# A two-layer hybrid decoder trunk on one core: maxima turned by grouped matmuls, three VectorE steps moved to ScalarE, pair halves of the residual norms summed before the ones-matmul

## The chip, the cores and the metric

The kernel runs on one core of one Trainium2 chip. The metric is the device time of one execution in microseconds. Before the change it is 1284.84 us, the median of three runs (1284.32 to 1285.02). The trace comes from one more execution, with the hardware profiler on; it took 1287.62 us, of which 1285.9 us lie between its first and last instruction (the span).

Engine names are those of the profile: PE is TensorE's matrix product and PEld its weight load, DVE is VectorE, ACT is ScalarE, POOL is GpSimd, SP is SyncE.

## What is computed

One sequence of 512 tokens and 16 meta tokens (L = 528), width 1024, two layers, everything in fp32. Each layer has a mixer and a feed-forward part, each between two RMS norms:

```python
def mixer_sublayer(h, ...):
    u = rms_norm(h, pre_g)
    z = jnp.einsum("bld,de->ble", u, w_in)
    q, k, v, f_logit, a_val, a_gate, sc_b, sc_c, sc_x = jnp.split(z, idx, axis=-1)
    log_f = jax.nn.log_sigmoid(f_logit + b_forget)
    y_attn = forgetting_attention(q, k, v, log_f)      # 8 heads of 64, causal softmax in query blocks
    a = a_val * jax.nn.sigmoid(a_gate)
    a = causal_depthwise_conv(a, a_dw_w) + a_dw_b      # 31 taps, 256 channels
    a = jax.nn.silu(layer_norm(a, a_ln_g, a_ln_b))
    y_conv = jnp.einsum("blc,ce->ble", a, a_pw_w)
    y_sc = sc_b * causal_depthwise_conv(sc_c * sc_x, sc_conv_w)   # 3 taps
    y = jnp.concatenate([y_attn, y_conv, y_sc], axis=-1)
    y = jnp.einsum("ble,ed->bld", head_rms_norm(y, head_g), w_out)
    return h + rms_norm(y, post_g)

def ffn_sublayer(h, ...):
    u = rms_norm(h, pre_g)
    z = causal_depthwise_conv(jnp.einsum("bld,df->blf", u, w_up), conv_w)   # 3 taps
    g, up = jnp.split(z, 2, axis=-1)
    return h + rms_norm(jnp.einsum("blf,fd->bld", jax.nn.silu(g) * up, w_down), post_g)
```

## The kernel before

Activations lie with channels on the 128 partitions and time along the free axis, in two time halves of H = 264 (`half_sl`). Every large product is done in three passes of a rounded type (`mm3`, L675): high part of the weights by high part of the activations, high by low, low by high. Weights stream from HBM in blocks of 128 output columns; ScalarE makes the high part (L629, L477 and L498) and VectorE the low part (L633, L478, L499).

The order of the instructions on every engine is mostly made at build time by a planner, `Flow`. It keeps a virtual clock for each engine. Threads (Python generators) issue the matmuls, and operations of the other engines are queued with a duration (`act_us`, `dve_us`, `stt_us`), what they come after, and a priority; whichever can start first on the virtual clocks goes out next. The durations decide the order alone; on the chip each engine runs its list in order and waits on semaphores. So a change of the operations of one stage also reorders the matmuls of that stage. The middle of the feed-forward part lies outside the planner and is ordered by the tile framework.

Places that matter below:

- **Maxima** (`maxima`, L1393). For each of the 8 heads, scores of queries by keys are made once more (L1407) to find the row maxima: VectorE reduces each piece along the free axis into one column of `mcol` (L1414), one column for each of five query blocks (`QB`: 16 queries, then four of 128). A maximum then stands on a partition for each query; the exponentials need it along the free axis, as one extra row of q (`mrow`) that meets a row of ones in k. The column is turned by a matmul with the identity (L1431): one matmul for each block, four in a first group and one in a second. ScalarE copies each group with a factor of -1 into the row of q (L1434): 400 elements, then 128.
- **Exponentials** (`logits`, L1453): two matmuls of k by q for each piece, the first of which reads the row of maxima; ScalarE takes exp of the result (L1462).
- **Fill.** The thread `fill` keeps TensorE busy between these with the input projections (`proj` and `v_proj`, L675 and L1259), later with the first output products (`Early`).
- **Convolution** (`conv_taps`): 31 taps on VectorE for two channel blocks; the first is a multiply and add of a scalar (L988), the others L991.
- **Short convolution** (`sc_x`): three steps on VectorE, the first a multiplication (L1069), then L1071 twice.
- **Layer norm and silu** (`conv_tail`, `silu`): gain (L1596), bias (L1599, VectorE), exp (L1600, ScalarE), ln, exp, and a product (L1603).
- **Residual norms** (`Norms`). `square` adds squares of channel blocks, two at a time, into `acc`, a tile of two halves of a block each (L763 and L772). `factor` sums over channels by a matmul with a matrix of 1/1024, `om_d` (L812, plain fp32), once for each of the two halves of the pair; three ScalarE steps (L822, L825, L826) and two of VectorE (L827, L833) make the factor. Key "y" is the norm behind a sublayer, "h" the one ahead of the next; each has two time halves (0 and 1). `post_norm` scales (L889), adds to h (L899) and writes the next input in two parts (L904 on ScalarE, L906 on VectorE). In the last sublayer the second half of "y" has its last blocks kept apart (`alone`).

Of the kernel before, what the change touches and what calls it, by code (L numbers as in the profile page):

```python
# [15 lines left out]
P = 128  # L16
# [310 lines left out]
def stt_us(n):  # L327
    return 0.22 + 0.00102 * n
# [13 lines left out]
def tile_hybrid_trunk(ctx: ExitStack, tc: tile.TileContext, xT, wflat, pv_d, out):  # L342
# [35 lines left out]
    for l in range(DEPTH):  # L378
        pv = T(const, [P, NPV], F32, f"pv{l}")
        (nc.gpsimd if l else nc.sync).dma_start(pv, pv_d[l])  # L380
        pg = T(const, [P, NGAIN], F32, f"pg{l}")
        nc.vector.tensor_scalar_mul(pg, pv[:, :NGAIN], -0.5)
        pvs.append((pv, pg))

    ident_r = T(const, [P, P], F32R, "ident_r")
    ident = ident_r.bitcast(F32)
# [349 lines left out]
    class Norms:  # L736
# [17 lines left out]
        def square(self, key, k, src, n, *after, prio=1):  # L754

            apart = self.alone.get(key, self.apart.get(key[0], 0))
            s = self.sums.setdefault(key, {"parts": {}})
            us = act_us(2 * n)
            box, slot = {}, Slot()

            def squares(tile):
                box["c"] = tile()
                nc.scalar.activation(box["c"], src, AF.Square)  # L763

            if k == 0:
                a = act(us, lambda: squares(lambda: T(self.pool, [P, 2, H], F32, "acc", 2)[:, :, :n]), *after,
                        prio=prio, takes=[(self.acc, slot)])
                s["acc"], s["at"] = box, a
            else:
                a = act(us, lambda: squares(lambda: self.c_tile(n)), *after, prio=prio, takes=[(self.c, slot)])  # L770
                if k < KD - 2 * apart:
                    s["at"] = dve(dve_us(2 * n), lambda: nc.vector.tensor_add(s["acc"]["c"], s["acc"]["c"], box["c"]),  # L772
                                  a, s["at"], prio=prio)
                    slot.close(s["at"])
            if k == 0 or k >= KD - 2 * apart:
                s["parts"][max(0, k // 2 - KD // 2 + apart + 1) if k else 0] = box, slot
                box["at"] = [a]
            if k == KD - 2 * apart - 2:
                s["acc"]["at"], s["acc"]["there"] = [s["at"]], True
            return a  # L780

# [179 lines left out]
                first.slot[hf, 2 * j + i].close(a, d)  # L961

    def mixer(l, ypool, first, close_first, spans, front, rz0_at):
        pv, pg = pvs[l]

        def col(name, j):
            return pv[:, _COLS[name] + j:_COLS[name] + j + 1]
# [17 lines left out]
        def tap(j, i):  # L985
            src = apads[j][:, i:i + L]
            if i == 0:
                nc.vector.tensor_scalar(conv[j], in0=src, scalar1=col("a_dw_w", CK * j),  # L988
                                        scalar2=col("a_dw_b", j), op0=ALU.mult, op1=ALU.add)
# [71 lines left out]
        def sc_x(j):  # L1061
# [4 lines left out]

            def shift(i):
                if i == 2:
                    nc.vector.tensor_scalar(t, in0=cx[:, 2:], scalar1=col("sc_w", 3 * j + 2), scalar2=None, op0=ALU.mult)  # L1069
                else:  # L1070
                    nc.vector.scalar_tensor_tensor(t, in0=cx[:, i:i + L], scalar=col("sc_w", 3 * j + i), in1=t,  # L1071
                                                   op0=ALU.mult, op1=ALU.add)

            def use(hf, ps, tok, rz=None):
                c = half_sl(hf)
                got.append(dve(dve_us(H), lambda: nc.vector.tensor_mul(cx[:, 2 + H * hf:2 + H * (hf + 1)], ps, t[:, c]),
                               tok, sc_at[j, "c", hf], prio=0))
                if hf:
                    d = got
                    for i in (2, 0, 1):  # L1080
                        d = [dve(stt_us(L), lambda i=i: shift(i), *d, prio=3)]
                    sc_at[j, "x"] = d[0]
                return [got[-1]]

# [308 lines left out]
        def maxima():  # L1393

            for hd in range(HEADS):
                yield [When(lambda: k_at.get(hd)), When(lambda: q_at[hd] if hd // 2 in k2_at else None),
                       When(lambda: gate_at.get(hd))] + ([When(lambda: begun.get(hd - 1))] if hd else [])
                q1, k1 = qh[hd % 4][0], kh[hd % 4][0]
                mcol = T(mp, [P, 6], F32R, "mcol", 2)
                col_at = []  # L1400
                for b, (qs, n) in enumerate(QB):
                    end = qs + n
# [17 lines left out]
                        slot.close(d)  # L1420
                        yield
                    col_at.append(d)
                mrow = rows(hd)[2]
                at = []
                for group in (QB[:4], QB[4:]):
                    yield [col_at[QB.index(g)] for g in group]
                    ps, slot = yield from bank("s1")
                    c0, c1 = group[0][0], group[-1][0] + group[-1][1]
                    for qs, n in group:
                        b = QB.index((qs, n))  # L1430
                        nc.tensor.matmul(ps[:1, qs - c0:qs - c0 + n], lhsT=mcol[:n, b:b + 1],  # L1431
                                         rhs=ident_r[:n, :n], start=True, stop=True)
                    tok = flow.mm(0.07 * len(group))
                    at.append(act(act_us(c1 - c0), lambda ps=ps, c0=c0, c1=c1: nc.scalar.activation(  # L1434
                        q1[mrow, c0:c1], ps[:1, :c1 - c0], AF.Copy, scale=-1.0), tok, prio=0))
                    slot.close(at[-1])
                    yield
                max_at[hd] = at

# [4 lines left out]
        def logits(hd, b, s0, s1):  # L1444
# [35 lines left out]
                p_at[hd, "all"] = [x for v in at.values() for x in v] + [p_sum[hd]]  # L1480
            return tok

        psums = [T(ap, [P, L - P], F32, f"psum{i}") for i in range(2)]
        p_sum, s_free = {}, {}
        att, acc_at, norm_at, norm_mm = {}, {}, {}, {}
# [85 lines left out]
        def conv_tail(blk):  # L1571
# [22 lines left out]
            def silu(j, c, box, mine, e):  # L1594
# [4 lines left out]
                f = dve(vs, lambda: nc.vector.tensor_scalar(n, in0=n, scalar1=col("a_ln_b", j), scalar2=None, op0=ALU.add), f)  # L1599
                g = act(us, lambda: nc.scalar.activation(s, n, AF.Exp, scale=-1.0), f)  # L1600
                g = act(us, lambda: nc.scalar.activation(s, s, AF.Ln, bias=c_one), g)
                g = act(us, lambda: nc.scalar.activation(s, s, AF.Exp, scale=-1.0), g)
                f = dve(vs, lambda: nc.vector.tensor_mul(n, n, s), g)  # L1603
# [307 lines left out]
        rz0_at = [norms.sums["h", 0]["r_at"]]  # L1911

    for l in range(DEPTH):
        pv, pg = pvs[l]
        final = l == DEPTH - 1

        t0 = N_META if final else 0
# [195 lines left out]
```

## Time and profile before

| | |
|---|---|
| median of three runs | 1284.84 us |
| the profiled execution | 1287.62 us |
| its span | 1285.9 us |
| mean granted TensorE clock | 0.996 |
| L1431, the turning of maxima | 80 matmuls |
| L812, sums over channels | 42 fp32 matmuls, recorded as 84 |
| L1434, copies of the maxima | 32, 12.1 us on ScalarE |

A row of the groups view reads: line, engine, operation, tiles out<-in, shapes and count | busy us, mean ns of one | idle us of the engine before it and what ended it. A row of the timeline reads: start in us from the span's start, duration, engine, line, operation, tiles, shapes, count. Durations of matmuls overlap, since TensorE is pipelined; what a matmul takes from the others is the distance from its start to the next one's start. A row of the windows view gives, for a stretch, the busy us of each engine with its number of instructions, then the granted clock, the DMA share and GB/s.

### The profile page before, as it was taken

The numbers are of one execution on the slowest core, as the hardware profiler recorded it, in microseconds if no ns is written. First come the engines' busy times: TensorE is split into PE (matmuls) and PEld (weight loads), VectorE is DVE, ScalarE is ACT, GpSimd is POOL, SyncE is SP. The second block draws the span as 40 slices with busy tenths as digits, with TensorE's granted clock in tenths as the row PEclk, the third lists the DMA queues.
The fourth block names the chain that finished last, engine by engine and source line by source line (L and its number), as shares of the span: only waits on it lengthen the run. The fifth ranks groups of instructions, "written<-read, shape, count | busy, mean of one in ns | idle before, by whom it ended". The sixth has DMA issues, their size and how long they took to land. (4 is left out here: it accounts for less than half of the span.)

```text
span 1285.9 us, 24315 instructions
## 1 busy us (share of the span) xinstructions
PE 1266.1 (98%) x9922; PEld 1215.7 (95%) x9922; DVE 894.5 (70%) x1563; ACT 610.3 (47%) x1144; POOL 112.5 (9%) x270
## 2 busy tenths in 40 slices
PE   8999999999999999999999999999999999999997
PEld 8998899999999999999999998999999799989996
DVE  7888886688743775677568887767876257637664
ACT  7256567756433443344453445676543333323453
POOL 1311210100000000000214222100000000000000
PEclk8999999999999999999999999999999999999999
DMA  6132214425644656664551552334132332243221
GB/s 224 50 101 68 61 50 149 159 72 192 235 145 159 208 189 233 212 211 135 213 199 54 165 161 71 121 113 161 34 99 83 99 99 87 72 121 88 88 72 66
DMA packets 55440, 164.57 MB, mean 128 GB/s; under 512 B 6352, under 2 KB 16720, under 8 KB 55328
## 3 DMA queue, kind: packets, MB, share of 16 engines
q1 hardware_dynamic: 41200, 109.56, 26.1%
q0 software_dynamic: 14128, 53.45, 12.9%
q8 instruction: 78, 1.28, 0.4%
q14 instruction: 34, 0.28, 0.1%
HBM read 131.17 MB, written 27.46 MB: 123 GB/s over the span
## 5 line engine op out<-in xcount | busy, mean ns | idle before, releaser
L675 PE MATMUL psum<-uhi,whi 128*128 128x264 f32 (+1 forms) x1936 | 452.0, 287 | 0.9 <-ACT uhi L1887 0.9
L675 PE MATMUL psum<-ulo,whi 128*128 128x264 f32 (+1 forms) x1936 | 445.2, 284 | 0.7 <-DVE ulo L1889 0.4
L675 PE MATMUL psum<-uhi,wlo 128*128 128x264 f32 (+1 forms) x1936 | 444.8, 283 | 0.0
L675 PEld LDWEIGHTS psum<-uhi,whi 128*128 128x128 f32 x1936 | 322.6, 188 | 3.3 <-ACT uhi L1887 1.1
L675 PEld LDWEIGHTS psum<-ulo,whi 128*128 128x128 f32 x1936 | 322.1, 188 | 2.4 <-DVE ulo L906 1.0
L675 PEld LDWEIGHTS psum<-uhi,wlo 128*128 128x128 f32 x1936 | 322.3, 189 | 0.0
L675 PE MATMUL psum<-yhi,whi 128*128 128x264 f32 (+3 forms) x888 | 249.4, 304 | 4.4 <-ACT whi L629 2.6
L675 PE MATMUL psum<-yhi,wlo 128*128 128x264 f32 (+3 forms) x888 | 246.7, 300 | 0.5 <-DVE wlo L633 0.5
L675 PE MATMUL psum<-ylo,whi 128*128 128x264 f32 (+3 forms) x888 | 246.3, 299 | 0.0
L477 ACT CAST whi<-raw 128x1024 fp32r<-128x1024 f32 (+1 forms) x110 | 113.1, 1030 | 183.8 <-PE psum L675 145.3
L478 DVE TENSOR_TENSOR wlo<-raw,whi 128x1024 fp32r<-128x1024 f32 (+1 forms) x110 | 131.8, 1200 | 65.3 <-ACT whi L477 63.5
L675 PEld LDWEIGHTS psum<-yhi,whi 128*128 128x128 f32 x888 | 160.1, 190 | 11.4 <-ACT whi L629 2.8
L675 PEld LDWEIGHTS psum<-yhi,wlo 128*128 128x128 f32 x888 | 160.4, 190 | 6.1 <-DVE wlo L633 0.8
L675 PEld LDWEIGHTS psum<-ylo,whi 128*128 128x128 f32 x888 | 160.5, 190 | 5.7
L1994 DVE SCALAR_TENSOR_TENSOR c<-z,pv,c 128x528 f32<-128x528 f32 (+1 forms) x176 | 132.0, 756 | 2.6
L621 POOL DMA_DIRECT2D raw<-in_w_dram x60 | 32.2, 538 | 918.6 <-DMA raw<-in_w_dram 361.2
L991 DVE SCALAR_TENSOR_TENSOR cacc<-apad,pv,cacc 128x528 f32<-128x528 f32 x120 | 87.3, 763 | 0.9
L633 DVE TENSOR_TENSOR wlo<-raw,whi 128x1024 fp32r<-128x1024 f32 (+2 forms) x64 | 75.3, 1197 | 15.1 <-ACT whi L629 14.9
L629 ACT CAST whi<-raw 128x1024 fp32r<-128x1024 f32 (+2 forms) x64 | 64.1, 1030 | 14.6 <-PE psum L675 8.3
L2004 ACT ACTIVATE c<-c 128x528 f32<-128x528 f32 (+1 forms) x44 | 28.1, 639 | 83.8 <-DVE c L1994 83.8
L2012 ACT CAST yhi<-c 128x528 fp32r<-128x528 f32 (+1 forms) x44 | 27.5, 626 | 84.4 <-DVE c L2008 84.3
L1992 ACT ACTIVATE c<-z,pv 128x528 f32<-128x528 f32 (+1 forms) x88 | 63.4, 727 | 0.1
(223 smaller groups left out, 1472.1 us busy)
## 6 DMA issues: line engine op xcount, KB each, us to landing
raw<-in_w_dram SPq DMA_DIRECT2D x116, 512.0 KB
raw<-in_w_dram POOLq DMA_DIRECT2D x44, 512.0 KB, 4.1
split_w<-whi SPq DMA_DIRECT2D x20, 512.0 KB
split_w<-wlo SPq DMA_DIRECT2D x20, 512.0 KB
whi<-split_w POOLq DMA_DIRECT2D x20, 512.0 KB, 4.6
wlo<-split_w POOLq DMA_DIRECT2D x20, 512.0 KB, 6.2
raw<-in_w_dram SPq DMA_DIRECT2D x20, 448.0 KB
raw<-in_w_dram POOLq DMA_DIRECT2D x12, 448.0 KB, 3.6
```

The lines of the kernel that those rows point to most:

```text
L477: nc.scalar.copy(hi[:, :sz], raw[:, :sz])
L478: nc.vector.tensor_sub(lo[:, :sz], raw[:, :sz], hi[:, :sz].bitcast(F32))
L621: nc.gpsimd.dma_start(to, src)
L629: nc.scalar.copy(box["hi"][:, :sz], box["raw"][:, :sz])
L633: nc.vector.tensor_sub(lo[:, :sz], box["raw"][:, :sz], box["hi"][:, :sz].bitcast(F32))
L675: nc.tensor.matmul(d, lhsT=w[a][:, k, cols], rhs=rhs(b, k, hf), start=start and i == 0 and p == 0, stop=stop and i == n - 1 and p == 2)
L991: nc.vector.scalar_tensor_tensor(conv[j], in0=src, in1=conv[j], scalar=col("a_dw_w", CK * j + i), op0=ALU.mult, op1=ALU.add)
L1992: nc.scalar.activation(dst, src[:, 2:2 + 2 * fw], AF.Copy, scale=wtap(2, t))
L1994: nc.vector.scalar_tensor_tensor(dst, in0=src[:, i:i + 2 * fw], scalar=wtap(i, t), in1=dst, op0=ALU.mult, op1=ALU.add)
L2004: silu = nc.scalar.activation(cs[0], cs[0], AF.Silu)
L2012: nc.scalar.copy(ghi, cs[0])
```

## The change

Six things change.

1. The matmul that turns maxima takes all columns of a group at once: `mcol` with four columns as weights and the whole identity as moving operand, so four rows come out, of which row e holds block e's maxima in full. The copies into q then take all n rows of one block's columns with a scale that is -1 on row e and 0 elsewhere (`minus`), into n rows of q instead of one; k has four rows of ones, and the sum over them in the score product gives the one that is not zero. There are five copies for a head instead of two, and two matmuls instead of five. `mcol` becomes two fixed tiles, cleared once by GpSimd.
2. The first convolution tap is a ScalarE activation.
3. So is the first step of the short convolution.
4. The layer norm's bias goes into the exp as its bias (`nb`, the negated bias), and into the product behind it, which becomes a three-operand instruction.
5. For the norms of key "y", except the one kept apart, VectorE adds the two halves of `acc` in one more instruction, and `factor` sends one half through `om_d`.
6. VectorE makes three small constants at the start.

```diff
+        nb = T(const, [P, 2], F32, f"nb{l}")
+        c = _COLS["a_ln_b"]
+        nc.vector.tensor_scalar_mul(nb, pv[:, c:c + 2], -1.0)
...
+    minus = T(const, [P, 4], F32, "minus")
+    nc.vector.tensor_scalar_mul(minus, ident[:, :4], -1.0)
...
             if k == KD - 2 * apart - 2:
+                if key[0] == "y" and key not in self.alone:
+                    both = s["acc"]
+                    s["at"] = dve(dve_us(n), lambda: nc.vector.tensor_add(
+                        both["c"][:, 0, :], both["c"][:, 0, :], both["c"][:, 1, :]), s["at"], prio=prio)
+                    s["acc"]["tiles"] = (0,)
...
             if i == 0:
-                nc.vector.tensor_scalar(conv[j], in0=src, scalar1=col("a_dw_w", CK * j),
-                                        scalar2=col("a_dw_b", j), op0=ALU.mult, op1=ALU.add)
+                nc.scalar.activation(conv[j], src, AF.Identity, scale=col("a_dw_w", CK * j), bias=col("a_dw_b", j))
...
-                    last[j] = dve(stt_us(L), lambda j=j, i=i: tap(j, i), last[j], prio=4 if i < CK - LATE else 0.5)
+                    last[j] = (dve if i else act)(stt_us(L), lambda j=j, i=i: tap(j, i), last[j],
+                                                  prio=(4 if i else 1) if i < CK - LATE else 0.5)
...
                 if i == 2:
-                    nc.vector.tensor_scalar(t, in0=cx[:, 2:], scalar1=col("sc_w", 3 * j + 2), scalar2=None, op0=ALU.mult)
+                    nc.scalar.activation(t, cx[:, 2:], AF.Copy, scale=col("sc_w", 3 * j + 2))
...
-            return slice(main, main + DH), slice(aux, aux + DH), slice(aux + 32, aux + 33)
+            return slice(main, main + DH), slice(aux, aux + DH), slice(aux + 32, aux + 36)
...
-                for group in (QB[:4], QB[4:]):
-                    yield [col_at[QB.index(g)] for g in group]
+                for b0, b1 in ((0, 4), (4, 5)):
+                    yield col_at[b0:b1]
                     ps, slot = yield from bank("s1")
-                    c0, c1 = group[0][0], group[-1][0] + group[-1][1]
-                    for qs, n in group:
-                        b = QB.index((qs, n))
-                        nc.tensor.matmul(ps[:1, qs - c0:qs - c0 + n], lhsT=mcol[:n, b:b + 1],
-                                         rhs=ident_r[:n, :n], start=True, stop=True)
-                    tok = flow.mm(0.07 * len(group))
-                    at.append(act(act_us(c1 - c0), lambda ps=ps, c0=c0, c1=c1: nc.scalar.activation(
-                        q1[mrow, c0:c1], ps[:1, :c1 - c0], AF.Copy, scale=-1.0), tok, prio=0))
-                    slot.close(at[-1])
+                    n = b1 - b0
+                    nc.tensor.matmul(ps[:n, :P], lhsT=mcol[:, b0:b1], rhs=ident_r, start=True, stop=True)
+                    tok = flow.mm(0.11)
+                    for b in range(b0, b1):
+                        qs, w = QB[b]
+                        at.append(act(act_us(w), lambda ps=ps, n=n, e=b - b0, qs=qs, w=w: nc.scalar.activation(
+                            q1[m0:m0 + n, qs:qs + w], ps[:n, :w], AF.Copy, scale=minus[:n, e:e + 1]), tok, prio=0))
+                    slot.close(*at[b0:b1])
...
-                f = dve(vs, lambda: nc.vector.tensor_scalar(n, in0=n, scalar1=col("a_ln_b", j), scalar2=None, op0=ALU.add), f)
-                g = act(us, lambda: nc.scalar.activation(s, n, AF.Exp, scale=-1.0), f)
+                g = act(us, lambda: nc.scalar.activation(s, n, AF.Exp, scale=-1.0, bias=nb[:, j:j + 1]), f)
...
-                f = dve(vs, lambda: nc.vector.tensor_mul(n, n, s), g)
+                f = dve(stt_us(H), lambda: nc.vector.scalar_tensor_tensor(
+                    n, in0=n, scalar=col("a_ln_b", j), in1=s, op0=ALU.add, op1=ALU.mult), g)
```

Since the planner orders by its virtual clocks, the change also moves other work. Two places follow.

TensorE's list at the fourth head of the first layer, where the maxima are turned and the first exponentials' products follow (L1431 turns the maxima, `mcol`; L1453 is the score product of that head, k by q; L1259 and L675 are fill; the changed kernel's lines are L1441, L1464 and L1271). Before:

```order
L675 MATMUL psum_67<-ulo_107,whi_1296 128x264
L675 MATMUL psum_67<-uhi_106,wlo_1325 128x264
L1431 MATMUL psum_67<-ident_r_76,mcol_1536 1x16
L1431 MATMUL psum_67<-ident_r_76,mcol_1536 1x128 x4
L1453 MATMUL psum_67<-q_106_687,k_98_679 128x16
L1453 MATMUL psum_67<-q_107_688,k_99_680 128x16
```

And in the changed kernel, where the list has L1441 with four columns, six matmuls of fill, L1441 with one column, three of fill, and then:

```order
L1271 MATMUL psum_67<-whi_1437,uhi_112 128x256
L1271 MATMUL psum_67<-whi_1437,ulo_113 128x256
L1271 MATMUL psum_67<-wlo_1454,uhi_112 128x256
L1271 MATMUL psum_67<-whi_1498,uhi_112 128x256
L1271 MATMUL psum_67<-whi_1498,ulo_113 128x256
L1271 MATMUL psum_67<-wlo_1561,uhi_112 128x256
L1464 MATMUL psum_67<-q_109_694,k_101_686 128x16
L1464 MATMUL psum_67<-q_110_695,k_102_687 128x16
```

Before, nothing stands between the turning and the score products that read its result; now nine matmuls of fill stand behind the second turning matmul, and six more behind the first.

VectorE's list in the first layer, at the end of the mixer's output product, where the squares of the second time half come to their sum (L772, acc; the changed kernel's L778, and L787 for its new sum of halves; L499 and L505 are a weight's low part). Before:

```order
L899 TENSOR_TENSOR h_2845<-h_2845,yp_2832 128x2x264
L889 TENSOR_TENSOR yp_2832<-yp_2832,rs_2842 128x2x264 x2
L499 TENSOR_TENSOR wlo_3537<-raw_3534,whi_3536 128x1024
L772 TENSOR_TENSOR acc_2887<-acc_2887,c_3230 128x528
L906 SCALAR_TENSOR_TENSOR ulo_107<-h_2845,pg_3_70,uhi_106 128x264 x2
```

And in the changed kernel:

```order
L900 TENSOR_TENSOR yp_2777<-yp_2777,rs_2787 128x2x264 x2
L505 TENSOR_TENSOR wlo_3535<-raw_3532,whi_3534 128x1024
L910 TENSOR_TENSOR h_2790<-h_2790,yp_2777 128x2x264
L778 TENSOR_TENSOR acc_2828<-acc_2828,c_3229 128x528
L917 SCALAR_TENSOR_TENSOR ulo_113<-h_2790,pg_3_70,uhi_112 128x264
L787 TENSOR_TENSOR acc_2828<-acc_2828 128x264
```

One more residual addition to h (L899, now L910) and one low part (L906, now L917) have come ahead of the complete sum, and the sum of halves is added.

More of the change, by code (lines that the diff above doesn't have):

```diff
@@ L963, in mixer @@
     def mixer(l, ypool, first, close_first, spans, front, rz0_at):
-        pv, pg = pvs[l]
+        pv, pg, nb = pvs[l]
         def col(name, j):
@@ L1080, in use @@
                     for i in (2, 0, 1):
-                        d = [dve(stt_us(L), lambda i=i: shift(i), *d, prio=3)]
+                        d = [act(act_us(L), lambda: shift(2), *d) if i == 2 else
+                             dve(stt_us(L), lambda i=i: shift(i), *d, prio=3)]
                     sc_at[j, "x"] = d[0]
@@ L1398, in maxima @@
                 q1, k1 = qh[hd % 4][0], kh[hd % 4][0]
-                mcol = T(mp, [P, 6], F32R, "mcol", 2)
+                mcol = mcols[hd % 2]
                 col_at = []
@@ L1422, in maxima @@
                     col_at.append(d)
-                mrow = rows(hd)[2]
+                m0 = rows(hd)[2].start
                 at = []
-                for group in (QB[:4], QB[4:]):
-                    yield [col_at[QB.index(g)] for g in group]
+                for b0, b1 in ((0, 4), (4, 5)):
+                    yield col_at[b0:b1]
                     ps, slot = yield from bank("s1")
-                    c0, c1 = group[0][0], group[-1][0] + group[-1][1]
-                    for qs, n in group:
-                        b = QB.index((qs, n))
-                        nc.tensor.matmul(ps[:1, qs - c0:qs - c0 + n], lhsT=mcol[:n, b:b + 1],
-                                         rhs=ident_r[:n, :n], start=True, stop=True)
-                    tok = flow.mm(0.07 * len(group))
-                    at.append(act(act_us(c1 - c0), lambda ps=ps, c0=c0, c1=c1: nc.scalar.activation(
-                        q1[mrow, c0:c1], ps[:1, :c1 - c0], AF.Copy, scale=-1.0), tok, prio=0))
-                    slot.close(at[-1])
+                    n = b1 - b0
[6 more added lines that the diff above has]
+                    slot.close(*at[b0:b1])
                     yield
@@ L1481, in logits @@
             return tok
+        mcols = [T(ap, [P, 6], F32R, f"mcol{i}") for i in range(2)]
+        for t in mcols:
+            mset(t, 0.0)
         psums = [T(ap, [P, L - P], F32, f"psum{i}") for i in range(2)]
@@ L1913, in tile_hybrid_trunk @@
     for l in range(DEPTH):
-        pv, pg = pvs[l]
+        pv, pg, nb = pvs[l]
         final = l == DEPTH - 1
```

2 lines of the change are left out of this document (1 added, 1 removed).

## The prediction

> **What bounds the kernel now.** I read the page's busy shares first, then who TensorE waits for, then the timeline where it waits.
>
> ```profile
> PE 1266.1 (98%) x9922; PEld 1215.7 (95%) x9922; DVE 894.5 (70%) x1563; ACT 610.3 (47%) x1144; POOL 112.5 (9%) x270
> PE psum L675 <- ACT whi L629: 2.6, 1, 2.6
> PE psum L1453 <- ACT q L1434: 1.0, 1, 1.0
> ```
>
> TensorE is busy 98% of the span, and its longest wait (2.6 us) is at the start, which the change leaves alone. The wait of 1.0 us for copies of maxima (L1434) is at a place that the change touches, and one more follows below. So the time is the sum of what TensorE issues, plus a few waits, and VectorE and ScalarE matter only where TensorE ends up waiting. I add up TensorE's issue, then look for places where another engine has the last word.
>
> **Maxima, TensorE's part.** The first head of the first layer, TensorE's timeline:
>
> ```profile
> 83.05 0.28 PE L675 MATMUL psum<-uhi,wlo 128*128 128x264 f32 x1
> 83.27 0.44 PE L1431 MATMUL psum<-ident_r,mcol 16*1 16x16 f32 x4
> 83.54 0.34 PE L675 MATMUL psum<-uhi,whi 128*128 128x264 f32 x1
> 83.71 0.29 PE L675 MATMUL psum<-ulo,whi 128*128 128x264 f32 x1
> ...
> 84.21 0.28 PE L675 MATMUL psum<-uhi,wlo 128*128 128x264 f32 x1
> 84.33 0.22 PE L1431 MATMUL psum<-ident_r,mcol 128*1 128x128 f32 x1
> 84.39 0.34 PE L675 MATMUL psum<-uhi,whi 128*128 128x264 f32 x1
> 84.56 0.28 PE L675 MATMUL psum<-ulo,whi 128*128 128x264 f32 x1
> ```
>
> A fill matmul takes 0.12 us from start to start (84.21 to 84.33). From 83.05 to 83.71 there are two such steps and the group of four, so the group costs 0.66 - 0.24 = 0.42 us. From 84.21 to 84.56 there are two and a single one: 0.35 - 0.24 = 0.11 us. The group's first member uses 16 partitions, and 83.05 to 83.27 shows 0.10 us lost ahead of it. The new matmuls use all 128 partitions and 128 moving columns, like the single one, so I price both at 0.11. A head goes from 0.53 to 0.22 us, so 16 heads save 5.0 us; in four heads the five stand together, where the single one costs only 0.06, so I take **4.8 us**. Bounds: 2.9 us (48 matmuls fewer at 0.06, the price of 84.33 to 84.39, the group's entry cost staying) and 5.0.
>
> **Norms, TensorE's part.** A sum over channels:
>
> ```profile
> 245.28 0.28 PE L675 MATMUL psum<-yhi,wlo 128*128 128x264 f32 x1
> 245.40 1.05 PE L812 MATMUL psum<-acc,om_d 128*128 128x264 f32 x4
> 246.09 0.48 PE L675 MATMUL psum<-yhi,whi 128*128 128x264 f32 x1
> 246.41 0.28 PE L675 MATMUL psum<-ylo,whi 128*128 128x264 f32 x1
> ```
>
> 245.28 to 246.41 less two steps of 0.12 is 0.89 us for the two halves, 0.445 each. Seven norms drop one half: 3.1 us. But VectorE adds one instruction (about 0.43 us, the price of L1603's 128x264 product below) ahead of the sum, and in the two mixers VectorE is full at that place:
>
> ```profile
> 255.00:275.00 20.00, 18.92 (x143) 17.86 (x141) 19.92 (x38) 13.15 (x30) 0.00 (x0) 1.00 0.31 106
> 895.00:910.00 15.00, 14.86 (x121) 14.43 (x119) 15.00 (x31) 10.01 (x24) 0.00 (x0) 1.00 0.01 1
> 634.00:649.00 15.00, 15.00 (x118) 14.74 (x117) 11.61 (x21) 9.52 (x20) 5.23 (x10) 1.00 0.82 286
> ```
>
> VectorE (third figure after the length) works 19.92 of 20 us behind the first mixer and 15.00 of 15 behind the second, and TensorE is the one with gaps. There the end of the stretch is VectorE's: the four halves that TensorE drops around there buy nothing, and an added 0.43 us pushes the end out, bounded by 0 and 0.43 for each mixer. I take 0.4 for the first and 0.2 for the second, since its sum stands at the stretch's edge. Behind the first feed-forward part VectorE has 3.4 us free of 15 and TensorE none, so two halves count in full, and so does the one of the last sublayer: 3 x 0.445 = 1.3. Net **0.7 us saved**, bounds +0.5 (only 0.4 of the 1.3 comes through) and -3.1.
>
> The wait of TensorE itself in the first mixer gets longer, though:
>
> ```profile
> 257.53 1.22 DVE L499 TENSOR_TENSOR wlo<-raw,whi 128x1024 fp32r<-128x1024 f32 x1
> 258.66 0.70 DVE L772 TENSOR_TENSOR acc<-acc,c 128x528 f32<-128x528 f32 x1
> 259.28 0.89 DVE L906 SCALAR_TENSOR_TENSOR ulo<-h,pg,uhi 128x264 fp32r<-128x264 f32 x2
> 259.42 1.16 PE L812 MATMUL psum<-acc,om_d 128*128 128x264 f32 x4 [0.94 <-DVE acc L772]
> ```
>
> In the new order an L899 (0.62, the step from 258.66 to 259.28 for the same size), one L906 (0.45, half of 0.89) and the new addition (0.43) also stand ahead: 1.5 us more, so the wait of 0.94 becomes about 2.5 to 2.9. What stands ahead no longer stands behind, so the end of this VectorE-bound stretch moves by the addition alone; that is the 0.4 above.
>
> **The wait at the fourth head and the half clock.** TensorE's timeline and the windows around it:
>
> ```profile
> 123.73 0.49 PE L1431 MATMUL psum<-ident_r,mcol 16*1 16x16 f32 x5
> 125.18 0.96 PE L1453 MATMUL psum<-q,k 128*128 128x16 f32 x4 [0.95 <-ACT q L1434]
> 124.10:127.50 3.40, 2.26 (x14) 1.59 (x11) 2.80 (x7) 3.03 (x8) 0.00 (x0) 1.00 0.35 80
> 127.50:130.95 3.45, 3.38 (x16) 3.30 (x17) 2.90 (x10) 1.08 (x4) 3.11 (x7) 0.51 0.46 151
> 258.20:261.60 3.40, 2.46 (x17) 2.11 (x16) 3.40 (x7) 0.90 (x3) 0.00 (x0) 1.00 0.84 294
> ```
>
> Here all five turning matmuls are followed at once by the products that need them. TensorE waits 0.95 us, is busy 2.26 us of 3.40, and then the granted clock falls to 0.51 for 3.45 us, which costs 1.7 us. Behind 258.20, busy 2.46 of 3.40, it did not fall. In the changed order fifteen fill matmuls (1.8 us) stand in this place, so both go: **1.0 + 1.7 = 2.7 us**. Bounds 0 and 2.7.
>
> The Trainium skill ("TensorE: Matmul & The Clock Gate", the section on the HAM clock gate) says that the clock halves after at least one idle window of about 3.4 us. The length of the slow stretch agrees with such a window, but no gap here is that long: the trace shows it falling after a stretch busy two thirds. By the page's rule the cause would lie elsewhere, the 1.7 us would stay, and the sum would be 1.7 less; that is the second rival's result.
>
> **ScalarE's added work.** The copies of the maxima, and what a column as operand costs:
>
> ```profile
> L1434 ACT ACTIVATE q<-psum 1x400 fp32r<-1x400 f32 x16 | 7.9, 493 | 14.6 <-PE psum L1431 10.0 <-DVE mcol L1414 3.3 <-DVE rs_t L1151 0.6
> L1434 ACT ACTIVATE q<-psum 1x128 fp32r<-1x128 f32 x16 | 4.2, 262 | 1.9 <-PE psum L1431 1.9
> L1529 ACT COPY yta<-psum 128x16 f32<-128x16 f32 x8 | 1.6, 196 | 0.0
> L1601 ACT ACTIVATE apad<-apad,c_one 128x264 f32<-128x264 f32 x8 | 3.8, 500 | 0.0
> L1600 ACT ACTIVATE apad<-cacc 128x264 f32<-128x264 f32 x8 | 3.1, 412 | 0.0
> 84.59 0.27 ACT L1434 ACTIVATE q<-psum 1x128 fp32r<-1x128 f32 x1 [0.31 <-PE psum L1431]
> 124.64 0.65 ACT L1434 ACTIVATE q<-psum 1x400 fp32r<-1x400 f32 x2
> ```
>
> Two copies were 0.755 us, or 0.65 in a row since they overlap by 0.1. L1601 has a column for its bias and L1600 none: 0.09 us apart at one size. So five copies are 0.20 + 4 x 0.262 + 5 x 0.09 = 1.70, or 1.3 in a row. The new order leaves 12 to 24 fill matmuls, 1.45 to 2.9 us, between the first turning matmul and the score products; a copy starts 0.26 us behind its matmul (84.33 to 84.59). So 1.55 us of chain stand against a cover of 1.45 or more: about 0.1 us is bare in the heads with short cover. Behind the copies in ScalarE's list wait exps and the high parts of k, which hold PSUM banks and are late by 0.65. Bounds: 0, and 0.93 x 16 = 14.9 us with no cover at all. I take **0.8 us lost**, near the covered end, because one of 16 waits was bare before.
>
> **The other edits**, all priced at nothing on the path:
>
> ```profile
> L988 DVE TENSOR_SCALAR cacc<-apad,pv 128x528 f32<-128x528 f32 x4 | 2.7, 678 | 0.0
> L1069 DVE TENSOR_SCALAR sccx<-cxp,pv 128x528 f32<-128x528 f32 x4 | 2.4, 597 | 0.1
> L1599 DVE TENSOR_SCALAR cacc<-cacc,pv 128x264 f32<-128x264 f32 x8 | 2.4, 351 | 0.0
> L1603 DVE TENSOR_TENSOR cacc<-cacc,apad 128x264 f32<-128x264 f32 x8 | 3.3, 427 | 0.2 <-ACT apad L1602 0.2
> L1992 ACT ACTIVATE c<-z,pv 128x528 f32<-128x528 f32 x44 | 32.0, 733 | 0.1
> ```
>
> VectorE loses 2.7 + 2.4 + 2.4 = 7.5 us, ScalarE gains eight activations of about 0.73 (L1992 is the same form), nearly all in the attention stages, where fill keeps TensorE busy. The moved steps now wait on ScalarE for VectorE's products (L958, L1076); queued behind them are the next gate's exps and the copies of v, which free PSUM banks. They start late by at most one such product, 0.4 us, eight times: 0 to 3 us lost, and 0 to 1 gained through VectorE. I take 0, since TensorE waits for none of these today. The three small constants fall in VectorE's idle time ahead of the first low part, and GpSimd, at 9%, clears two small tiles more; wider rows of q and k change no length.
>
> **Sum**: -4.8 - 0.7 - 2.7 + 0.8 = -7.4 us against the profiled execution's 1287.62. That one lies 2.8 us above the median of the runs; the terms are differences, so I carry them over to 1284.84: **1277.4 us**, 0.58% faster. Its own range, from the smaller bounds, is 1275.5 to 1279.5.
>
> **Rivals.**
>
> *First: the copies come late.* TensorE waits at every head as it does at the fourth. For it: ScalarE's chain grows from 0.65 to 1.3 us, in order with everything else. Against: one bare wait in 16 before, and a planned cover as long as the chain. Bare everywhere, it costs 14.9 instead of 0.8: 1291.5, **slower**. It decides from (7.4 + 0.8) / 16 = 0.5 us of bare wait a head; at half of that 1281.3, at 0.4 us about 1283.0, no change. Chances: slower 0.05, no change 0.06, faster all the same 0.04.
>
> *Second: the half clock stays*, here or at the longer wait behind the first mixer, where TensorE's busy share falls well below the two thirds of above. It costs 1.7 to 2.7 us: 1279.1 to 1280.1; two such stretches 1282.5, about no change. Chances 0.19 and 0.04.
>
> *Third: the turning matmul doesn't save what it should*, because the loss at a group's entry belongs to waiting for `mcol` and not to 16 partitions: 2.9 for 4.8, giving 1279.3. For it: one loss at each group. Against: the single matmul reads `mcol` too and shows none. Chance 0.12.
>
> **How the numbers follow.** Forecast 0.50. 0.2% is about what measurements of this kernel can tell from no change. Faster: 0.50 + 0.19 + 0.12 + 0.04 = 0.85; within 0.2%: 0.06 + 0.04 = 0.10; slower 0.05. For the range: all bounds together at their best (-5.0 - 3.1 - 2.7) give 1274.0; the high end takes in the second and third rival and the first at 0.35 us a head, 1282.7.
>
> **What would show it.** L1441 at 32 matmuls, each 0.06 to 0.11 us from its neighbours; L812's successor at 35 sums, recorded as 70; a clock of 1.00 around 127 us; the wait ahead of the first mixer's second sum at 2.5 us or more, and VectorE full behind it. Many waits of L1464 for L1445 would make the prediction wrong, as would a half clock in new places.

## The result, and the profile after

| | before | after |
|---|---|---|
| median | 1284.78 us (4 runs, 1284.32 to 1285.02) | 1293.55 us (4 runs, 1292.30 to 1294.72) |
| ratio | | 1.0068, 95% interval 1.0052 to 1.0084 |
| the profiled execution, its span | 1287.62 us, 1285.9 us | 1292.30 us, 1290.6 us |

The changed kernel is 0.7% slower; forecast was 0.6% faster. The two profiled executions lie only 4.7 us apart, the medians 8.8: before's profiled execution lies 2.8 us above its median (about 1 us of that is a weight block that landed late, shown under the norms below), and after's lies 1.25 below. So the difference of the two profiles understates the loss. A row of the windows view gives a stretch's length, then busy time (and instructions) of TensorE, its weight loads, VectorE, ScalarE and GpSimd, then TensorE's granted clock, DMA share and GB/s. Before:

```profile
200.00:225.00 25.00, 25.00 (x195) 24.47 (x194) 15.59 (x37) 18.19 (x48) 1.32 (x6) 1.00 0.39 129
```

After:

```profile
124.10:127.50 3.40, 3.40 (x32) 3.33 (x31) 3.37 (x10) 1.65 (x6) 0.46 (x2) 1.00 0.28 85
127.50:131.00 3.50, 3.50 (x29) 3.20 (x28) 2.18 (x9) 2.09 (x7) 1.38 (x4) 1.00 0.29 75
200.00:225.00 25.00, 18.80 (x115) 16.68 (x114) 14.61 (x34) 17.02 (x45) 1.27 (x6) 0.87 0.41 129
```

Around 124 us the wait and the half clock are gone, as forecast. The loss stands at 200 to 225 us, the end of the first layer's attention: TensorE issues 115 matmuls there where it issued 195, and the clock falls. The waits of TensorE (in all, how many, the longest) name who it waits for:

```profile
PE psum L681 <- ACT yhi L1180: 3.2, 2, 2.3
PE psum L681 <- DVE rs_t L1163: 2.4, 1, 2.4
PE psum L681 <- ACT whi L635: 2.2, 1, 2.2
PE psum L681 <- DVE ylo L1181: 2.0, 1, 2.0
```

Only the third was there before (2.6 us at the start). The second is a single wait in the second layer, at 850.73 us. The first and the last are products of the output projection (y) that wait for the norms of the mixer's last channels, each computed from a sum on TensorE (`bd`), three steps of ScalarE, two of VectorE (L1163, L1166), a gain, and the split into a high (L1180) and a low part (L1181). TensorE's timeline in the first layer; the bracket is the wait:

```profile
211.02 0.28 PE L681 MATMUL psum<-yhi,wlo 128*128 128x264 f32 x1
212.05 0.71 PE L1579 MATMUL psum<-sq,bd 128*128 128x264 f32 x2 [0.75 <-DVE rs_t L1163]
213.58 0.39 PE L681 MATMUL psum<-yhi,whi 128*128 128x264 f32 x1 [0.82 <-ACT yhi L1180]
...
218.00 0.39 PE L681 MATMUL psum<-yhi,whi 128*128 128x264 f32 x1 [2.35 <-ACT yhi L1180]
220.40 0.59 PE L681 MATMUL psum<-ylo,whi 128*128 128x264 f32 x1 [2.02 <-DVE ylo L1181]
```

And VectorE's:

```profile
202.63 0.77 DVE L1163 SCALAR_TENSOR_TENSOR rs_t<-psum,rs_t 128x264 f32<-128x264 f32 x2 [4.94 <-ACT rs_t L1162]
206.88 0.77 DVE L1163 SCALAR_TENSOR_TENSOR rs_t<-psum,rs_t 128x264 f32<-128x264 f32 x2 [0.89 <-ACT rs_t L1162]
211.23 0.77 DVE L1163 SCALAR_TENSOR_TENSOR rs_t<-psum,rs_t 128x264 f32<-128x264 f32 x2 [0.89 <-ACT rs_t L1162]
215.47 0.77 DVE L1163 SCALAR_TENSOR_TENSOR rs_t<-psum,rs_t 128x264 f32<-128x264 f32 x2 [0.79 <-ACT rs_t L1162]
...
217.65 2.35 DVE L639 TENSOR_TENSOR wlo<-raw,whi 128x1024 fp32r<-128x1024 f32 x2
219.93 0.42 DVE L1181 TENSOR_TENSOR ylo<-cacc,yhi 128x264 fp32r<-128x264 f32 x1
```

Four pairs of norms go one behind the other, 4.3 us each, and VectorE is not full meanwhile: ahead of each pair it waits for ScalarE's steps. Ahead of the last low parts stand two low parts of weights (L639, 2.35 us), which makes the last wait, 2.02. The waits of TensorE's rows add up to 5.9 us. From 220.40 to 225.40 us it then works at half clock, which costs some 2.5 us more (an estimate: half of that time).

### The profile page after: what moved, and what is told of

It reads as the page before. It is cut to its first block, busy times and chain, and to the rows that moved or that the text cites. A ratio compares the mean times of both kernels' runs of the same rounds, so it can differ in the third digit from the quotient of the medians.

```text
span 1290.6 us, 24254 instructions
## 1 busy us (share of the span) xinstructions
PE 1262.1 (98%) x9860; PEld 1211.1 (94%) x9860; DVE 889.3 (69%) x1557; ACT 626.1 (49%) x1200; POOL 112.0 (9%) x274
## 5 line engine op out<-in xcount | busy, mean ns | idle before, releaser
L639 DVE TENSOR_TENSOR wlo<-raw,whi 128x1024 fp32r<-128x1024 f32 (+2 forms) x64 | 75.4, 1197 | 16.5 <-ACT whi L635 16.0
```

Of the source, the lines that this page charges most:

```text
L639: nc.vector.tensor_sub(lo[:, :sz], box["raw"][:, :sz], box["hi"][:, :sz].bitcast(F32))
```

## The experiments

All results, with the comparison of each against runs of before on the same chip. The last three columns are the first layer's: F, matmuls of the input projection left behind the last weighing product; A, those and the ones of the output projection up to the last norm sum (both from TensorE's list); and TensorE's busy time with its clock from 200 to 225 us.

| run | median, us | ratio to before, interval | F | A | busy, clock |
|---|---|---|---|---|---|
| before | 1284.6 to 1285.3 | | 36 | 123 | 25.00, 1.00 |
| after | 1293.55 | 1.0068, 1.0052 to 1.0084 | 3 | 75 | 18.80, 0.87 |
| e1_max | 1278.66 | 0.9949, 0.9934 to 0.9964 | 21 | 111 | 25.00, 1.00 |
| e2_act | 1294.36 | 1.0069, 1.0053 to 1.0086 | 6 | 78 | 21.16, 0.90 |
| e3_norm | 1285.22 | 1.0000, 0.9990 to 1.0009 | 36 | 123 | 25.00, 1.00 |
| e4_both_in_place | 1285.07 | 1.0000, 0.9991 to 1.0010 | 36 | 123 | 25.00, 1.00 |
| e5_act_old_order | 1284.68 | 0.9995, 0.9985 to 1.0004 | 36 | 123 | 25.00, 1.00 |
| e6_new_order_only | 1293.57 | 1.0067, 1.0051 to 1.0084 | 6 | 78 | 19.87, 0.85 |
| e7_all_old_tail | 1278.25 | 0.9945, 0.9930 to 0.9960 | 21 | 111 | 25.00, 1.00 |
| e8_max_order_only | 1282.88 | 0.9983, 0.9973 to 0.9992 | 21 | 111 | 25.00, 1.00 |
| e9_tap | 1286.15 | 1.0010, 1.0000 to 1.0020 | 27 | 105 | 24.79, 1.00 |
| e10_shift | 1286.03 | 1.0010, 1.0001 to 1.0019 | 36 | 132 | 25.00, 1.00 |
| e11_bias | 1293.30 | 1.0063, 1.0048 to 1.0078 | 36 | 81 | 21.08, 0.93 |
| e12_held_back | 1290.79 | 1.0042, 1.0027 to 1.0057 | 48 | 81 | 21.95, 0.93 |
| e13_pw_after_norm | 1284.12 | 0.9993, 0.9984 to 1.0003 | 3 | 102 | 21.82, 0.93 |
| e14_pw_after_sum | 1279.05 | 0.9952, 0.9937 to 0.9967 | 3 | 93 | 24.81, 1.00 |

### The parts alone: e1 to e4

e1, e2 and e3 are before with one part of the change each: the maxima; first tap, first step of the short convolution (the shift) and bias; the norm halves.

> Only the maxima are turned by one matmul per group; first tap, shift, bias and norm sums stay as before. Theory T1 (the loss of the changed kernel comes from the steps moved to ScalarE, which let the last norms of the first layer's attention fall together): no stall there, last piece of the stretch (first sum over channels, 245.4 us before) 2 to 5 us earlier, in all 1278 to 1281 us. Rival T2 (the maxima's new order uses up the input projection's matmuls too early and so opens the stall): a stall of 5 us or more with half clock between 205 and 225 us, in all 1286 to 1292 us. Rival T3 (norm sums on VectorE cost it): as T1, 1278 to 1281 us.

> Only first tap, shift and layer norm bias go to ScalarE. T1: waits of TensorE of 5 us or more between 205 and 225 us and a stretch of half clock behind them, 8 to 12 us slower than before, 1293 to 1297 us. T2 and T3: within 2 us of before, no such stall.

> Only the pair halves of the residual norms are summed on VectorE. T1 and T2: 0 to 1.5 us faster than before (1283.3 to 1284.8 us); seven matmuls of 0.445 us gone, those of the two mixers given back. T3: slower than before by 3 us or more, with longer waits of TensorE at the sums over channels in both mixers.

The maxima alone gain 6.5 us, the moved steps alone lose 9.2, the norm sums do nothing (1285.22 us, 0.4 above T1's range and well under T3's 3 us). So T2 and T3 fall. The parts don't add up: -6.5 + 9.2 + 0.1 is 2.8, and the whole change loses 8.8. That speaks for something that the parts share. In e4, each new group of instructions is issued by one step of the planner at the cost of the step that it replaces, so the lists are before's but for the dropped matmuls:

```diff
-                    tok = flow.mm(0.11)
-                    for b in range(b0, b1):
-                        qs, w = QB[b]
-                        at.append(act(act_us(w), ...
+                    tok = flow.mm(0.07 * n)
+                    def turned(...):
+                        for b in range(b0, b1): nc.scalar.activation(...)
+                    at.append(act(act_us(sum(w for _, w in QB[b0:b1])), turned, tok, prio=0))
```

> Maxima by one matmul per group and norm halves summed on VectorE, with the order of every engine otherwise as before (no step moved to ScalarE). T1 and T2: all the saved issue of TensorE comes through, 4 to 6 us faster than before (1279 to 1281 us), with the wait at the fourth head's copies still there. T3: no faster than 1282 us.

T1 and T2 were wrong here: no gain at all. (T3's number fits, its reason does not, since e3 costs nothing.) Its groups (instructions | busy us, mean ns | idle time ahead, and who ended it) say why:

```profile
L1467 PE MATMUL psum<-q,k 128*128 128x16 f32 (+2 forms) x192 | 38.5, 299 | 2.6 <-ACT q L1447 2.3 <-ACT p L1476 0.2
...
L1516 PE MATMUL psum<-p,vals 128*64 128x16 f32 (+4 forms) x192 | 21.2, 366 | 0.6 <-ACT q L1447 0.6
```

The first row's products had 1.1 us of idle time in before, 1.0 of it for the copies, and have 0.0 in e1. Five copies instead of two are late where the list leaves nothing between the turning and its readers: with 0.5 us at a third place, TensorE waits 3.4 us for copies in e4. Against e3, which has the same norm sums, e4 falls back 0.9 us over the first layer's attention and gains 0.3 over the second's, so all of what the shorter turning saves goes back: 2.4 us of it in these waits, the rest in places that were not singled out. The norm halves bring nothing by themselves either, as e3 shows; its window and TensorE's timeline behind the first feed-forward part:

```profile
661.00:680.00 19.00, 17.72 (x134) 16.91 (x133) 12.29 (x24) 10.72 (x24) 1.23 (x4) 1.00 0.20 67
670.60 0.39 PE L675 MATMUL psum<-ulo,whi 128*128 128x264 f32 x1 [0.57 <-DVE ulo L862]
677.63 0.39 PE L675 MATMUL psum<-uhi,whi 128*128 128x264 f32 x1 [0.71 <-DVE apad L963]
```

Before, the same window reads:

```profile
661.00:680.00 19.00, 19.00 (x146) 18.39 (x146) 12.26 (x24) 11.18 (x26) 1.23 (x4) 1.00 0.20 62
```

TensorE had no gap there and now has 1.28 us of them, for two halves that it no longer sums (2 x 0.445 = 0.89); from 640 to 700 us e3 falls back 0.7 us against before. VectorE is busy 12.3 of 19 us in both, so it isn't full; but TensorE, with less to sum, now waits for VectorE's low parts (L862) and until its gated products have been read out of PSUM (L963).

### Order or work: e5 to e8

In e5 the moved steps run on ScalarE but are booked as VectorE's; in e6 it is the other way about. TensorE's list in e5 is before's, and in e6 it is e2's, line by line.

```diff
e5, against e2:
-                        d = [act(act_us(L), lambda: shift(2), *d) if i == 2 else dve(stt_us(L), ...
+                        d = [dve(stt_us(L), lambda i=i: shift(i), *d, prio=3)]
e6, against before:
-                        d = [dve(stt_us(L), lambda i=i: shift(i), *d, prio=3)]
+                        d = [act(act_us(L), lambda: shift(2), *d) if i == 2 else dve(stt_us(L), ...
```

The first tap and the bias likewise (in e5 the dropped addition keeps an empty step of the planner; in e6 the addition is issued together with the gain).

> First tap, shift and layer norm bias run on ScalarE, but the planner still books them as VectorE's at their old costs, so that the order of TensorE's work is that of before. If the loss of e2 (9.2 us) comes from the order that the planner draws up once these steps are ScalarE's: no stall at the end of the first attention, 1283.5 to 1286.5 us. If it comes from the work itself on ScalarE (its copies and squares late, norms late behind them): 1290 to 1296 us as in e2.

> The instructions of before, with every step on VectorE as it was, in the order that the planner drew up for e2. If the order makes the loss: waits of TensorE of 5 us or more between 205 and 225 us, half clock behind them, 1292 to 1297 us. If the work on ScalarE makes it: 1284 to 1287 us.

1284.68 and 1293.57: the work on ScalarE, in before's order, costs nothing that can be measured, and the order alone, with not one instruction changed, costs the whole 0.7%. e6's waits and its window at the place:

```profile
PE psum L675 <- ACT yhi L1170: 2.4, 2, 1.6
PE psum L675 <- ACT whi L629: 2.2, 1, 2.2
PE psum L675 <- DVE ylo L1171: 1.8, 1, 1.8
200.00:225.00 25.00, 19.87 (x126) 17.64 (x125) 15.21 (x37) 17.34 (x48) 1.27 (x6) 0.85 0.32 106
```

e7 is the changed kernel with e5's edit, and e8 the counterpart of e4: before's five matmuls and two copies a head, booked as the new ones (`flow.mm(0.11)` for `flow.mm(0.07 * len(group))`, and the sum of the single copies' costs).

> The whole changed kernel, with the steps moved to ScalarE booked as VectorE's, so that TensorE's order is that of e1 with one half fewer in each norm sum. If the order makes the loss: as e1 or up to 1 us less, 1277 to 1279.5 us. If the work on ScalarE makes it: 1286 us or more.

> The instructions of before (five turning matmuls and two copies a head), in the order that the planner draws up for one matmul per group. If e1's 6.5 us come in two parts, issue saved (4.8) and cover for the copies (2.7 at the fourth head, less late copies): 1.5 to 3.5 us faster than before, 1281.6 to 1283.6 us, with no wait at the fourth head. If the order does it all: 1278 to 1280 us. If the order does nothing: 1285 us.

Both came as expected. e7 is the changed kernel's work without the order's loss, and it beats before by 0.55%. Where the two part can be read off the first sums over channels behind each mixer, in the changed kernel:

```profile
250.61 0.61 PE L823 MATMUL psum<-acc,om_d 128*128 128x264 f32 x2
...
850.73 0.38 PE L681 MATMUL psum<-yhi,whi 128*128 128x250 f32 x1 [2.35 <-DVE rs_t L1163]
...
886.45 0.58 PE L823 MATMUL psum<-acc,om_d 128*128 128x250 f32 x2
```

and in e7:

```profile
241.09 0.61 PE L823 MATMUL psum<-acc,om_d 128*128 128x264 f32 x2
873.37 0.58 PE L823 MATMUL psum<-acc,om_d 128*128 128x250 f32 x2
```

9.5 us are lost by the end of the first mixer, 13.1 by the end of the second; the second holds one wait of the same family, for a norm sum to be read out of PSUM (L1163). The spans differ by 13.8 us.

### Which property of the order: e9 to e14

e9, e10 and e11 are before with only the first tap, the shift or the bias moved.

> Only the first tap goes to ScalarE. Between the last weighing product of the first layer and the last norm sum of its attention, the order has 27 products of the input projection left (before 36, e2 6) and 78 of the output projection: 105 in all (before 123, e1 111, e2 78, changed kernel 75). Theory F (it is the input projection's products left that decide): no stall, 1284 to 1286.5 us. Theory A (it is all cover up to the last norm sum, with about 110 to 120 needed): a stall of 0.5 to 2 us, 1285.5 to 1288 us.

> Only the shift goes to ScalarE. 36 products of the input projection are left, 132 in all to the last norm sum. Theories F and A: no stall, 1284 to 1286.5 us. If a moved step as such made the loss, whatever the order: 1287 us or more here or in e9 or e11.

> Only the layer norm bias is folded into ScalarE's exp. 36 products of the input projection are left after the last weighing product, but 24 of them stand behind the norms of the convolution, and all cover up to the last norm sum (here that of the short convolution) is 81. Theory F: no stall, 1283.5 to 1286.5 us. Theory A: a stall of 4 to 6 us in the first layer, 1290 to 1295 us.

The bias alone, which adds no instruction to ScalarE, makes nearly the whole loss; theory F falls with it, and A holds. e9 does not tell them apart: 1286.15 us lies in both ranges, and 0.2 us without a matmul at the place is less of a stall than A asked for. But the wait in e11 is of another kind than A had in mind. TensorE's timeline:

```profile
206.10 0.61 PE L1184 MATMUL psum<-apad,bd 128*128 128x264 f32 x2
209.63 0.59 PE L678 MATMUL psum<-uhi,whi 128*128 128x264 f32 x1 [2.92 <-DVE rs_t L1154]
```

An input projection's product, whose operands have long been there, waits until VectorE has read a norm sum out of PSUM. Six norm sums (`bd`) are issued there from 201.69 to 206.10 us; I read this as sums issued close together holding the banks that the next products need, which no run tests by itself. The 0.1% that e9 and e10 lie above before has, in e10 at least, no stall to go with it; I leave it open. e12 is the changed kernel with its last block of the input projection held back in the first layer:

```diff
             for hf in range(2):
+                if last and hf == 0:
+                    yield [When(lambda: p_at.get((HEADS - 1, "all")))]
                 d, slot = yield from bank("mm")
```

> The changed kernel, but in the first layer the last block of the input projection (48 products) waits for the last head's exps, so 48 of its products are left after the last weighing product (changed kernel 3); all cover to the last norm sum is 81. Theory F: the stall between 205 and 225 us goes, and with it 6 to 10 us, 1283 to 1288 us, less what the attention loses earlier for want of these products. Theory A: a stall of 4 to 6 us stays, 1290 to 1294 us.

6 of the 8.8 us of loss stay, and F falls again. e13 and e14 hold back the pointwise products of the convolution instead, whose four blocks feed two of the four last pairs of norms:

```diff
e13:
-                yield ends
+                yield ends + [When(lambda: norm_at.get(HEADS // 2 - 1))]
e14:
-                yield ends
+                yield ends + [When(lambda: norm_at[HEADS // 2 - 1][-1:] if HEADS // 2 - 1 in norm_at else None)]
```

> The changed kernel with every edit in it, but the convolution's 24 pointwise products (L1636) wait until the norm of the last attention pair is done; only 3 products of the input projection are left after the last weighing product, as in the changed kernel. Theory B (the last norms of the attention come in one bunch because the pointwise products stand ahead of the last attention pair's norm, and run one pair after another): the stall between 200 and 225 us is under 2.5 us, the one at 848 us is gone, and the time is 1277 to 1281.5 us. If the products of the input projection used up too early are the cause: the stall stays, 1288 us or more. If the work moved to ScalarE is: the same, 1288 us or more.

> As e13, but the pointwise products wait only until the last attention pair's squares have been summed on TensorE. Theory B: as e13, 1277 to 1282 us, since the last attention pair's norm still goes ahead of the convolution's. Otherwise: 1288 us or more.

e14 came as expected: with every edit in it, every one of the moved steps on ScalarE, and only three products of the input projection left, it is 0.5% faster than before. Its window:

```profile
200.00:225.00 25.00, 24.81 (x194) 24.11 (x194) 17.09 (x37) 20.35 (x49) 1.64 (x7) 1.00 0.37 129
```

e13 missed its range by 2.6 us, though it undoes most of the loss. Its timeline:

```profile
204.19 0.28 PE L681 MATMUL psum<-yhi,wlo 128*128 128x264 f32 x1
206.77 0.39 PE L681 MATMUL psum<-yhi,whi 128*128 128x264 f32 x1 [2.29 <-ACT yhi L1180]
208.04 0.59 PE L681 MATMUL psum<-ylo,whi 128*128 128x264 f32 x1 [0.89 <-DVE ylo L1181]
```

Held until the norm is done, the 24 products are missing as cover while TensorE waits for that norm. In e14 they may go once its sum is issued, and in its timeline they stand between 200.4 and 207.2 us, among products of y. That also breaks A as a count: e13 has 102 and stalls, e14 has 93 and does not. What decides seems to be what TensorE has in hand at each moment of the norms' chain, and whether their sums hold the banks; no single count that I tried gives it. That the order makes the loss is shown; which property of it does is shown only as far as e14 undoes it.

## Why the prediction was wrong

**The step that failed** is the one under "the other edits": "They start late by at most one such product, 0.4 us, eight times: 0 to 3 us lost, and 0 to 1 gained through VectorE. I take 0, since TensorE waits for none of these today." As to the work this was right: e5 runs it on ScalarE and measures 0.9995. What it left out is that the planner decides by booked costs and engines, so that moving a few steps draws up another list for TensorE, and the list that came out runs dry at the end of both attentions. The same instructions cost 1278.25 us in e7 and 1293.55 in the changed kernel: some 15 us for the order alone, more than any term of the sum. That "fill keeps TensorE busy" held for the middle of the attention and not for its end, which I did not look at. No rival had it either; the bound of 3 us was one on delays, not on lists. Of its signs of being wrong, "a half clock in new places" did appear.

**Maxima on TensorE, -4.8: right.** The changed kernel's rows at the first head:

```profile
82.52 0.28 PE L681 MATMUL psum<-uhi,wlo 128*128 128x264 f32 x1
82.72 0.22 PE L1441 MATMUL psum<-ident_r,mcol 128*4 128x128 f32 x1
82.78 0.33 PE L681 MATMUL psum<-uhi,whi 128*128 128x264 f32 x1
...
L1441 PE MATMUL psum<-ident_r,mcol 128*4 128x128 f32 (+1 forms) x32 | 7.1, 222 | 0.0
```

32 matmuls, 0.06 us to the next one. The 0.20 us from start to start ahead of this one, where a fill matmul takes 0.12, recurs once behind a fill matmul (at 726.95 us); the others have 0.11 to 0.13 there and lose nothing. Added up as in the prediction, all turnings take 8.2 us in e8 and 3.5 in e1, which has the same list: 4.7 us less. In medians, each against its own runs of before, e1 gains 6.5 and e8 2.4, which is 4.1 apart. The third rival does not hold.

**The fourth head, -2.7: right.** Wait and half clock are gone in the windows from 124.10 on, and e8, where only the list differs, is 2.4 us faster than before (0.9983). But the 1.7 us of half clock is not paid by every execution: nine traces have the wait at this place (0.95 us, 1.03 in e4), and in two of them, e6 and e9, no half clock follows.

**Copies on ScalarE, +0.8: too much.** The exponentials' products have no idle time for copies in e1 or in the changed kernel. The first rival's mechanism exists: e4, with before's list, waits 3.4 us for copies, 2.3 of it ahead of the exponentials' products. The new list covers it. No run leaves all 16 heads bare, so the 14.9 us for that is not tested. (By the terms of the sum, this rival at half of 0.5 us a head comes to 1280.7 us and not 1281.3, and at 0.35 us to 1282.2 and not 1282.7.)

**Norms, -0.7 net: the size was off.** e3 measures 1.0000 (0.9990 to 1.0009), which does not exclude 0.7. But "two halves count in full" behind the first feed-forward part is wrong: 1.28 us of new gaps stand against them. The wait ahead of the first mixer's second sum, forecast at 2.5 to 2.9, is short:

```profile
263.18 0.71 PE L823 MATMUL psum<-acc,om_d 128*128 128x264 f32 x2 [0.68 <-DVE acc L787]
```

The forecast started from 0.94 us of wait, and that belonged to one execution. In before's trace a weight block landed late, and the engines behind it came late with it; in e5, whose lists there are the same, the sum follows without a wait. First two rows of before, then one of e5:

```profile
248.09 1.05 ACT L629 CAST whi<-raw 128x1024 fp32r<-128x1024 f32 x1 [1.12 <-DMA raw<-in_w_dram]
249.17 1.23 DVE L633 TENSOR_TENSOR wlo<-raw,whi 128x1024 fp32r<-128x1024 f32 x1 [2.16 <-ACT whi L629]
...
258.28 1.16 PE L815 MATMUL psum<-acc,om_d 128*128 128x264 f32 x4
```

The new instructions make a wait of 0.5 us in e3 and in e7; why the 1.5 us more in the changed kernel's list show as no more than 0.68, no run singles out.

**The sum of the parts that I priced was right**: -7.4 forecast, 7.0 measured in e7 (1285.29 to 1278.25), the list's loss being the one thing left out of it. In part that is luck: the 0.8 us of the copies and the 0.7 of the norms, neither of which the runs show, cancel. **The second rival** said that the half clock stays. It went at its old place and came at a new one for 6.8 us, as a consequence of the stall and not as its cause.

## What to carry to other kernels

Where a planner makes the order, an edit of costs or engines is a new order everywhere. Walk through the bottleneck engine's new list from end to end, above all where a stage ends and cover is scarce, and price each place where it could wait for a chain of other engines; two or three places are not enough. To tell order from work on the chip, run the new instructions in the old order and the old instructions in the new one: here that took two runs, and it is also how to keep a gain (e7) that the planner's redrawing would have taken away.

## What was not expected of the hardware

The clock halves in windows of about 3.41 us, and it halves behind a window in which TensorE was busy for part of the time. In the changed kernel:

```profile
211.76:215.17 3.41, 2.22 (x12) 1.61 (x13) 2.59 (x7) 2.05 (x7) 0.00 (x0) 1.00 0.02 5
215.17:218.58 3.41, 0.87 (x5) 0.45 (x4) 3.11 (x7) 3.09 (x6) 0.00 (x0) 1.00 0.00 0
218.58:221.99 3.41, 1.59 (x7) 1.59 (x8) 2.11 (x4) 1.36 (x3) 1.27 (x6) 0.50 0.45 148
221.99:225.40 3.41, 3.41 (x17) 3.41 (x17) 0.22 (x1) 2.65 (x5) 0.00 (x0) 0.50 0.55 160
```

Five matmuls (0.87 us) in a window did not keep it up, and one full window at half clock brought it back, while 2.22 us of 3.41 (from 211.76) did not bring it down. The busy share alone is not the whole rule. In the window that holds the fourth head's wait, TensorE was busy for the same 2.27 us in e3 and in e6, and the clock fell behind it in e3 alone (e6's window starts 28 window lengths ahead of its later fall, at 217.68 us). In e3:

```profile
122.91:126.32 3.41, 2.27 (x16) 1.59 (x16) 2.58 (x8) 2.83 (x7) 0.00 (x0) 1.00 0.36 81
126.32:129.73 3.41, 3.41 (x17) 3.32 (x17) 3.06 (x11) 1.38 (x4) 2.44 (x5) 0.50 0.34 103
```

In e6:

```profile
122.12:125.53 3.41, 2.27 (x17) 1.59 (x17) 2.58 (x8) 2.58 (x7) 0.00 (x0) 1.00 0.32 72
125.53:128.94 3.41, 3.32 (x24) 3.03 (x25) 3.06 (x9) 1.80 (x5) 2.28 (x5) 1.00 0.27 69
```

The Trainium skill ("TensorE: Matmul & The Clock Gate", the section on the HAM clock gate) gives a free-running window of 3413 ns, and the lengths here agree; it says the clock falls after at least one idle window, and here no window was without matmuls. So short waits cost twice: of the 6.8 us at half clock in the changed kernel, TensorE works through the 5.0 from 220.40 us on, which adds some 2.5 us to the waits.
